# Loads of an attention unit issued one per step of attention

## The chip, the cores and the metric

One core of a Trainium2 chip runs the whole kernel in one launch. The metric is the device time of that launch in microseconds (us); lower is better. The kernel before has a median of 2948.92 us over three runs.

## The reference

One layer of a transformer trunk on 2048 tokens of width 1024, in float32. The changed part belongs to the token mixer:

```python
h = rms_norm(x, g_attn[l]) * (1.0 + scale_a) + shift_a
proj = h @ w_in[l]
q_f, k_f, v_f, q_s, k_s, v_s, f_logit = jnp.split(proj, offsets, axis=-1)
log_f = jax.nn.log_sigmoid((f_logit + b_fgate[l]).astype(jnp.float32))
o_fox = forgetting_attention(...)        # 8 heads of 64: softmax(q.k/8 + F[t] - F[s]), s <= t
o_sb = stick_breaking_attention(...)     # 8 heads of 64: sigmoid(z) * prod of (1 - sigmoid(z)), s < t
mix = jnp.concatenate([head_rms_norm(o_fox, ...), head_rms_norm(o_sb, ...)], axis=-1)
x = x + gate_a * (mix @ w_out[l])
```

Behind it come a gated MLP of inner width 2752 (1024 x 8/3, rounded to 64) with a causal convolution of width 3, and a final RMSNorm. The gates, shifts and scales come from `silu(c) @ w_ada + b_ada`.

## The kernel before

**Precision.** Every operand of a matrix product is split into a high and a low part (fp32r), and a product is three matmuls: high-high, high-low, low-high. A tile therefore has a dimension of two, and most loads carry both parts.

**Units.** Attention is cut into 32 units `(kind, p, tb)`: the kind (`sb`, stick-breaking, then `fox`, forgetting), a pair of heads p from 0 to 3, and a block tb of 512 queries from 0 to 3. A unit needs its own queries Q, and the keys K and values V of its own block and of all earlier blocks of its pair. The units run in that order, one after the other. `attend(...)` is a generator: each of its steps writes one piece of a unit (logits on PE at L596 and L597, the elementwise part on DVE, ACT and POOL, transposes on PE at L606, weighted values on PE at L615). A unit has between 11 and 47 steps.

**Projections.** The projection of a unit (generator `ahead`, function `proj`) reads the eight tiles of normalised input `hs[tb][kt]` from DRAM into tiles named hp (L468, 512 KB each) and multiplies them on PE (L342 for Q and K, L413 for V). In `finish_proj` the results go to DRAM: Q and K into one tensor `qk_...` (L380, L394), V into `vs_...` (L440). Later they are read back by `load_unit` as a unit's tiles: four loads of Q (L362, 256 KB each), four of K (L363, 128 KB each), one of V (L364, 512 KB). The detour through DRAM lays the two parts of both heads out over the partitions as the logits want them. The very first block of the first pair is filled directly.

**Buffers.** Q has 2 buffers, K 5 and V 5. The tiles named hp have 10, shared by the projection's input, by the loads of `w_ada` and by the tiles of its sum.

**Interleaving.** While unit i is attended, `follow(m)` is called at each of its steps m. It advances the projections to a goal that `pace(i)` sets, and once the next unit has been projected it loads that unit. From unit 12 on, `late_mod` is mixed in as well: it loads blocks of `w_ada` (L776), scales them on ACT (L782), sums them on POOL (L783), reduces the sum on PE (L790, L800) and writes one gate to DRAM (`gate_m`, L796).

**What sets the order on each engine.** The kernel is written in the Tile framework, and the context is opened like this:

```python
with _tile.TileContext(nc, schedule_with_timeline_sim=True) as tc:
```

With that option the framework does not issue instructions in program order. A list scheduler with a timeline of its own picks the next instruction of each engine; program order is a priority among those that are ready in that timeline. Only parts that are marked (`fixed()`, `tc.issue_after`) keep a given order. All loads and stores named here are issued by one queue, SP (`nc.sync`), in order: an instruction that waits holds up those behind it. Each DMA on SP also takes one of eight semaphores in turn, so it can be issued only when the DMA eight places ahead of it has landed.

**Names in the profile.** Tiles appear under their names without buffer numbers: `K<-qk_fox` is the load of a K tile, `hp<-hs` a load of the projection's input, `hp<-in_w_ada_dram` a load of w_ada, `os<-oT` the write of a unit's output, `ps_pj`, `ps_qk`, `ps_pt`, `ps_pv` the banks of PSUM for projections, logits, transposes and weighted values.

## Time and profile before

| | us |
|---|---|
| median of three runs | 2948.92 |
| lowest, highest | 2948.36, 2949.31 |
| profiled execution, span from the first to the last instruction | 2941.4 |
| its own total time | not listed |
| PE (matmul) busy | 2867.8 (97%) |
| VectorE (DVE) busy | 2179.5 (74%) |
| ScalarE (ACT) busy | 1686.0 (57%) |
| GpSimd (POOL) busy | 901.1 (31%) |

The span leaves out what lies ahead of the first and behind the last instruction; against the median that is 7.5 us. Rows of the timeline give a start, a duration, the engine (SPq is the SP queue that issues DMAs; its time is the issuing, not the transfer), the line, the operation, the tiles and a count, and in brackets how long the engine had been idle and what ended that. Rows of stretches give for each engine the busy time and the instructions, then the granted clock of PE (1.00 is full), the busy share of the DMA engines and the bytes moved in GB/s.

### The profile page before, as it was taken

Reading aid. Unit: us, or ns where it says so; the run is one execution under the profiler, and the core shown is the slowest. Engines: PE = TensorE matmul, PEld = TensorE weight load, DVE = VectorE, ACT = ScalarE, POOL = GpSimd, SP = SyncE. Lnnn points to the kernel's source line nnn. Section 1 sums busy time; section 2 is a strip of 40 time slices with the busy share of each in tenths; the row PEclk is TensorE's granted clock in tenths of the full one; section 3 lists DMA queues with packets and bytes.
Section 4 is the critical chain, followed back from the end, with each engine's and each line's share of the span. In section 5 each row is a group of like instructions: output and inputs, shape, how many; then the busy total and the mean of one; then the engine's idle time right before and its main releaser. Section 6 shows DMA issues by size and latency. Waiting matters only on the chain.

```text
span 2941.4 us, 45922 instructions
## 1 busy us (share of the span) xinstructions
PE 2867.8 (97%) x15772; PEld 2459.7 (84%) x15772; DVE 2179.5 (74%) x3464; ACT 1686.0 (57%) x3187; POOL 901.1 (31%) x967
## 2 busy tenths in 40 slices
PE   8999999999999999999999999999999999999998
PEld 7888888888988988888888788888788888888887
DVE  5787778877886656658843788888998888575476
ACT  5776767677776656658744554444444445433342
POOL 0431322243032423231213344444254543142200
PEclk8999999999999999999999999999999999999999
DMA  9749756867469794794537775554754444975644
GB/s 293 255 139 321 236 188 207 301 211 229 162 212 356 269 277 139 232 323 140 182 120 233 245 232 128 130 136 129 236 132 125 130 130 132 309 257 185 216 158 151
DMA packets 348346, 601.89 MB, mean 205 GB/s; under 512 B 34672, under 2 KB 178800, under 8 KB 348112
## 3 DMA queue, kind: packets, MB, share of 16 engines
q1 hardware_dynamic: 324208, 558.06, 57.7%
q0 software_dynamic: 10880, 20.97, 4.3%
q10 hardware_dynamic: 13024, 19.93, 1.9%
q8 instruction: 124, 2.03, 0.3%
q14 instruction: 110, 0.90, 0.1%
HBM read 420.77 MB, written 177.02 MB: 203 GB/s over the span
## 4 chain that ended last, share of the span: by engine, by line
PE 46%; DMA 3%; DVE 2%; SPq 1%; ACT 1%; issue 1%; POOL 0%; DVEq 0%; ACTq 0%; POOLq 0%
PE ps_o L1315 19%; PE ps_t L1315 7%; PE ps_o L1614 6%; PE ps_t L1614 3%; PE ps_bc L1614 3%; PE ps_o L912 1%; PE ps_pv L615 1%; DMA r<-rstd 1%; PE ps_bc L912 1%; PE ps_pt L606 1%; PE ps_o L1609 1%; DMA wo<-wos 1%; DMA hm<-hf_m 1%; SPq L895 1%; DVE op L46 1%
## 5 line engine op out<-in xcount | busy, mean ns | idle before, releaser
L1315 PE MATMUL ps_o<-op,wu 128*128 128x512 f32 x2592 | 608.0, 389 | 2.0 <-DVE snap L1366 1.5
L1315 PEld LDWEIGHTS ps_o<-op,wu 128*128 128x128 f32 x2592 | 486.2, 188 | 103.9 <-DVE snap L1366 1.9
L611 DVE TENSOR_TENSOR at<-ps_pt,at 128x512 fp32r<-128x512 f32 (+1 forms) x576 | 366.1, 652 | 100.2 <-ACT at L610 97.3
L636 DVE TENSOR_TENSOR_SCAN a<-r,a 128x512 f32<-128x512 f32 (+2 forms) x320 | 368.3, 1167 | 77.8 <-ACT a L631 39.9
L342 PE MATMUL ps_pj<-hp,w_qk 128*128 128x512 f32 x1512 | 411.2, 403 | 14.5 <-DMA hp<-hs 12.9
L610 ACT ACTIVATE at<-ps_pt 128x512 fp32r<-128x512 f32 (+1 forms) x576 | 318.5, 576 | 139.1 <-PE ps_pt L606 123.1
L615 PE MATMUL ps_pv<-at,V 128*128 128x256 f32 x2216 | 386.8, 292 | 9.3 <-DVE at L611 4.2
L615 PEld LDWEIGHTS ps_pv<-at,V 128*128 128x128 f32 x2216 | 320.9, 190 | 39.8 <-DVE at L611 11.4
L342 PEld LDWEIGHTS ps_pj<-hp,w_qk 128*128 128x128 f32 x1512 | 275.4, 190 | 71.0 <-DMA hp<-hs 16.2
L45 ACT ACTIVATE wu<-wuraw 128x512 fp32r<-128x512 f32 x204 | 128.9, 632 | 248.5 <-PE ps_o L1315 190.1
L596 PE MATMUL ps_qk<-K,Q 128*128 128x512 f32 (+2 forms) x640 | 265.7, 416 | 5.6 <-ACT a L631 3.3
L413 PE MATMUL ps_pj<-w_v,hp 128*128 128x256 f32 (+1 forms) x1536 | 236.6, 288 | 2.1 <-DVE hp L422 1.6
L597 PE MATMUL ps_qk<-K,Q 128*128 128x512 f32 (+2 forms) x640 | 235.7, 369 | 0.0
L1315 PE MATMUL ps_t<-op,wu 128*128 128x512 f32 x888 | 220.8, 390 | 1.0 <-DVE op L46 1.0
L413 PEld LDWEIGHTS ps_pj<-w_v,hp 128*128 128x128 f32 x1536 | 209.0, 189 | 10.9 <-DVE q L373 1.5
L630 ACT ACTIVATE r<-ps_qk 128x512 f32<-128x512 f32 (+2 forms) x320 | 173.1, 541 | 58.2 <-PE ps_qk L597 55.5
L46 DVE TENSOR_TENSOR wu<-wuraw,wu 128x512 fp32r<-128x512 f32 x204 | 189.6, 930 | 18.1 <-ACT wu L45 16.7
L1315 PEld LDWEIGHTS ps_t<-op,wu 128*128 128x128 f32 x888 | 166.4, 188 | 36.5 <-DVE op L46 1.8
L606 PE MATMUL ps_pt<-edge,a 128*128 128x128 f32 x1088 | 185.1, 274 | 8.4 <-DVE a L636 7.8
L1614 PE MATMUL ps_o<-op 128*128 128x512 f32 x840 | 191.5, 389 | 0.0
L1614 PEld LDWEIGHTS ps_o<-op 128*128 128x128 f32 x840 | 157.7, 188 | 32.7
L679 ACT ACTIVATE p<-p,mn 128x128 f32<-128x128 f32 (+15 forms) x128 | 153.9, 1203 | 53.3 <-DVE mn L675 52.2
(342 smaller groups left out, 5237.6 us busy)
## 6 DMA issues: line engine op xcount, KB each, us to landing
hp<-hs SPq DMA_DIRECT2D x224, 512.0 KB
wuraw<-in_w_up_dram SPq DMA_DIRECT2D x80, 512.0 KB
ra<-g SPq DMA_DIRECT2D x136, 256.0 KB
rb<-in_w_down_dram SPq DMA_DIRECT2D x108, 256.0 KB
g<-u SPq DMA_DIRECT2D x80, 256.0 KB
hs<-hp SPq DMA_DIRECT2D x32, 512.0 KB
hp<-in_w_ada_dram SPq DMA_DIRECT2D x32, 512.0 KB
qk_fox<-q SPq DMA_DIRECT2D x32, 512.0 KB
```

Source lines behind the costliest of these rows:

```text
L46: (lo_engine or nc.gpsimd).tensor_sub(lo, src, f(hi))
L342: nc.tensor.matmul(acc, w[kt][:, a, n], h[:, bb], start=kt == 0 and i == 0, stop=kt == KT - 1 and i == 2)
L413: nc.tensor.matmul(av[:, t * width:(t + 1) * width], hts[kt][:, a, tok], w[1][kt][:, bb, 0:width], start=kt == 0 and m == 0, stop=kt == KT ...
L596: nc.tensor.matmul(b[:, :cw], Q[:, hl, 0, qcols], K[:, hl, :cw], start=True, stop=False)
L597: marks.append(nc.tensor.matmul(b[:, :cw], Q[:, hl, 1, qcols], K[:, hl, :cw], start=False, stop=True).ins)
L606: nc.tensor.transpose(b[:, i * P:(i + 1) * P], blk(kts[kk], qi), ident)
L610: copies = [nc.scalar.activation(at[:, 0, lo:], b[:, lo:], AF.Copy).ins, nc.vector.tensor_sub(at[:, 1, lo:], b[:, lo:], f(at[:, 0, lo:])).ins]
L611: nc.vector.tensor_sub(at[:, 1, lo:], b[:, lo:], f(at[:, 0, lo:])).ins]
L615: m = nc.tensor.matmul(o[:, 0:2 * P], V[kt // 4][:, kt % 4, hl, :], rhs, start=first and kk == 0 and w == 0, stop=last and kk == 1 and w == 1)
L636: nc.vector.tensor_tensor_scan(rev, r[:, 0:need][:, ::-1], rev, 0.0 if right[qi] is None else right[qi][:, 0:1], ALU.mult, ALU.add)
L1315: nc.tensor.matmul(b, w[:, p, j], o[:, q], start=first and i == 0, stop=last and i == 2, skip_group_check=True)
L1614: nc.tensor.matmul(b, a[:, p, t * P:(t + 1) * P], w[:, q], start=first and i == 0, stop=last and i == 2, skip_group_check=True)
```

## The change

`load_unit` no longer issues its nine loads. It appends them to a list `arriving`, in the same order as before. A new function `arrive(n)` issues the first n of the list. `follow` calls it at every step: with one load, as long as more than six steps beyond those that the list needs are left in the unit, and with the whole list otherwise.

```diff
@@ load_unit
             for r in range(2):
                 half = slice(r * HD, (r + 1) * HD)
-                nc.sync.dma_start(f(Q[half, h]), src[rows, 0])
-                nc.sync.dma_start(f(K[half, h]), src[rows, 1, r])
-        nc.sync.dma_start(f(V), vs[kind][p][tb])
+                arriving.append((f(Q[half, h]), src[rows, 0]))
+                arriving.append((f(K[half, h]), src[rows, 1, r]))
+        arriving.append((f(V), vs[kind][p][tb]))
         res.append((Q, K, V))
+
+    arriving = []
+
+    def arrive(n):
+        for _ in range(min(n, len(arriving))):
+            nc.sync.dma_start(*arriving.pop(0))
@@ ahead of the loop over the units
     load_unit(*units[0], results["sb", 0])
+    assert not arriving
@@ follow(m), in the loop over the units
             if nxt and projected[1] > i + 1 and loaded_units[0] == i + 1:
                 loaded_units[0] += 1
                 load_unit(*nxt, results[nxt[:2]])
+            arrive(1 if n - m > len(arriving) + 6 else len(arriving))
```

Nothing else is changed. In the kernel after, the three load lines are one, L371, and lines behind it stand 6 to 8 further down (L468 is L474, L596 is L602, L606 is L612, L615 is L621, L740 is L746, L776 is L782, L796 is L802).

**What moves.** Both kernels issue 1775 DMAs on SP. In the schedule, 20 of them stand at another place: five loads of K, five of hp<-hs, three writes at L394, two loads of w_ada, two of the MLP's weights, and one each at L380, L740 and L1443. Of the 252 loads of Q, K and V, the other 247 keep their place. On PE the first 6372 matmuls stand as before, those between 1045.8 and 1332.7 us of the profile before are partly reordered, then again a few between 2104.8 and 2163.9 us.

The first place is SP near 1041 to 1052 us of the profile before, while the first FoX unit is attended. `hs_5`, `hs_6` and `hs_7` are the last three input tiles of a projection that PE is in the middle of; `qk_fox_3_12746` holds the keys of a later unit. Before:

```order
L363 DMA K<-qk_fox_3_12746 64x512 x4
L468 DMA hp<-hs_5_73 128x1024
L468 DMA hp<-hs_6_74 128x1024
L468 DMA hp<-hs_7_75 128x1024
L776 DMA hp<-in_w_ada_dram 128x1024
L363 DMA K<-qk_fox_0_13205 64x512 x4
```

After:

```order
L371 DMA K<-qk_fox_3_12746 64x512 x2
L474 DMA hp<-hs_5_73 128x1024
L371 DMA K<-qk_fox_3_12746 64x512
L474 DMA hp<-hs_6_74 128x1024
L474 DMA hp<-hs_7_75 128x1024
L371 DMA K<-qk_fox_3_12746 64x512
L782 DMA hp<-in_w_ada_dram 128x1024
L371 DMA K<-qk_fox_0_13205 64x512 x4
```

The load of hs_5 has moved ahead of two of the four K loads.

PE at the same place, around the six matmuls that use hs_5 (L342). Before:

```order
L606 MATMUL ps_pt<-edge,p 128x128 x3
L615 MATMUL ps_pv<-at,V 128x256 x5
L596 MATMUL ps_qk<-K,Q 128x384
L597 MATMUL ps_qk<-K,Q 128x384
L596 MATMUL ps_qk<-K,Q 128x512
L597 MATMUL ps_qk<-K,Q 128x512
L342 MATMUL ps_pj<-hp,w_qk 128x512 x6
L606 MATMUL ps_pt<-edge,p 128x128
```

After:

```order
L612 MATMUL ps_pt<-edge,p 128x128 x3
L621 MATMUL ps_pv<-at,V 128x256 x5
L342 MATMUL ps_pj<-hp,w_qk 128x512 x6
L602 MATMUL ps_qk<-K,Q 128x384
L603 MATMUL ps_qk<-K,Q 128x384
L602 MATMUL ps_qk<-K,Q 128x512
L603 MATMUL ps_qk<-K,Q 128x512
L612 MATMUL ps_pt<-edge,p 128x128
```

The six projection matmuls have moved ahead of four logits matmuls.

The second place is SP near 1195 to 1204 us. `hs_7_91` is the last input tile of a projection, `gate_m` is the write of the gate. Before:

```order
L362 DMA Q<-qk_fox_1_14178 64x1024 x3
L363 DMA K<-qk_fox_2_14948 64x512
L796 DMA gate_m<-hp 128x1024
L363 DMA K<-qk_fox_2_14948 64x512
L468 DMA hp<-hs_7_91 128x1024
L364 DMA V<-vs_fox_1_223 128x1024
```

After:

```order
L371 DMA Q<-qk_fox_1_14178 64x1024 x3
L474 DMA hp<-hs_7_91 128x1024
L802 DMA gate_m<-hp 128x1024
L371 DMA K<-qk_fox_2_14948 64x512 x2
L371 DMA V<-vs_fox_1_223 128x1024
```

The load of hs_7 has moved ahead of two K loads and the write of gate_m.

PE at the second place, around the six matmuls that use hs_7. Before:

```order
L606 MATMUL ps_pt<-edge,p 128x128 x4
L615 MATMUL ps_pv<-at,V 128x256 x3
L606 MATMUL ps_pt<-edge,p 128x128 x4
L615 MATMUL ps_pv<-at,V 128x256 x4
L606 MATMUL ps_pt<-edge,p 128x128 x4
L615 MATMUL ps_pv<-at,V 128x256 x5
L606 MATMUL ps_pt<-edge,p 128x128 x3
L342 MATMUL ps_pj<-hp,w_qk 128x512 x6
L615 MATMUL ps_pv<-at,V 128x256 x3
```

After:

```order
L612 MATMUL ps_pt<-edge,p 128x128 x4
L342 MATMUL ps_pj<-hp,w_qk 128x512 x6
L621 MATMUL ps_pv<-at,V 128x256 x3
L612 MATMUL ps_pt<-edge,p 128x128 x4
L621 MATMUL ps_pv<-at,V 128x256 x4
L612 MATMUL ps_pt<-edge,p 128x128 x4
L621 MATMUL ps_pv<-at,V 128x256 x4
L612 MATMUL ps_pt<-edge,p 128x128 x3
```

The six have moved ahead of 23 transposes and value matmuls (11 and 12).

The third place is PE near 1281 to 1288 us, where the projection of a later unit begins; its first four hp loads keep their places on SP. Before:

```order
L615 MATMUL ps_pv<-at,V 128x256 x4
L606 MATMUL ps_pt<-edge,p 128x128 x3
L615 MATMUL ps_pv<-at,V 128x256 x3
L606 MATMUL ps_pt<-edge,p 128x128 x2
L596 MATMUL ps_qk<-K,Q 128x256
L597 MATMUL ps_qk<-K,Q 128x256
L342 MATMUL ps_pj<-hp,w_qk 128x512 x12
L615 MATMUL ps_pv<-at,V 128x256
```

After:

```order
L602 MATMUL ps_qk<-K,Q 128x512
L603 MATMUL ps_qk<-K,Q 128x512
L612 MATMUL ps_pt<-edge,p 128x128 x6
L602 MATMUL ps_qk<-K,Q 128x256
L603 MATMUL ps_qk<-K,Q 128x256
L342 MATMUL ps_pj<-hp,w_qk 128x512 x18
L602 MATMUL ps_qk<-K,Q 128x512
L603 MATMUL ps_qk<-K,Q 128x512
```

The matmuls of the new projection's first three hp tiles, which open the twelve, now stand among the eighteen; 27 matmuls of attention that ran ahead of them (9 transposes, 12 of values, 6 of logits) now run behind them.

Two smaller places have no table here. Near 1062 to 1081 us SP issued a load of w_ada, then the two writes of L380 and L394, another load of w_ada, the write at L740 and eight loads hp<-hs; after, it issues the two writes, the first of those w_ada loads, the write, the other w_ada load and then the hp loads. Near 2105 to 2164 us, at the end of a half of the MLP, DVE and ACT run a few operations in another order.

## The prediction

> **What bounds the kernel now.** The page first: its totals and its chain of waits.

> ```profile
> span 2941.4 us, 45922 instructions
> PE 2867.8 (97%) x15772; PEld 2459.7 (84%) x15772; DVE 2179.5 (74%) x3464; ACT 1686.0 (57%) x3187; POOL 901.1 (31%) x967
> PE 46%; DMA 3%; DVE 2%; SPq 1%; ACT 1%; issue 1%; POOL 0%; DVEq 0%; ACTq 0%; POOLq 0%
> ```

> TensorE works 2867.8 of 2941.4 us; all its idle time is 73.6 us. A changed load order pays or costs only where PE waits for a load. So the second view is what PE waited for (line, wait, us in total, times, longest):

> ```profile
> PE ps_pj L342 <- DMA hp<-hs: 12.9, 8, 6.0
> ...
> PE ps_o L1315 <- DVE snap L1366: 1.5, 1, 1.5
> ...
> PE ps_t L1315 <- DVE op L46: 1.0, 1, 1.0
> ...
> PE ps_qk L596 <- DMA K<-q: 0.7, 1, 0.7
> ...
> PE ps_o L1315 <- DVE op L46: 0.5, 1, 0.5
> ```

> No row has PE waiting for the unit loads of L362 to L364; the one wait for a K is on the first unit, which the projection fills directly. The loads that do make PE wait are hp<-hs, the projection's input, on the same SP queue. The third view, PE in order of time, has two of those waits at 6.01 and 3.40 us, 9.4 of the 12.9:

> ```profile
> 1045.81 0.34 PE L596 MATMUL ps_qk<-K,Q 128*128 128x384 f32 x1
> ...
> 1046.39 0.40 PE L597 MATMUL ps_qk<-K,Q 128*128 128x512 f32 x1
> 1052.80 2.93 PE L342 MATMUL ps_pj<-hp,w_qk 128*128 128x512 f32 x6 [6.01 <-DMA hp<-hs]
> ...
> 1086.71 0.71 PE L342 MATMUL ps_pj<-hp,w_qk 128*128 128x512 f32 x2
> ...
> 1156.69 0.39 PE L596 MATMUL ps_qk<-K,Q 128*128 128x512 f32 x1
> ...
> 1202.54 0.60 PE L615 MATMUL ps_pv<-at,V 128*128 128x256 f32 x3
> ...
> 1208.81 2.93 PE L342 MATMUL ps_pj<-hp,w_qk 128*128 128x512 f32 x6 [3.40 <-DMA hp<-hs]
> ...
> 1280.71 0.39 PE L596 MATMUL ps_qk<-K,Q 128*128 128x512 f32 x1
> ...
> 1284.27 2.91 PE L342 MATMUL ps_pj<-hp,w_qk 128*128 128x512 f32 x12
> ```

> Each wait has a second price, seen in stretches of time (us; busy us of PE, PEld, DVE, ACT, POOL; granted clock; DMA share; GB/s). The first four rows are the waits and what follows them; the others lie on a grid of 3.41 us:

> ```profile
> 1046.79:1052.80 6.01, 0.00 (x1) 0.00 (x0) 0.98 (x5) 1.79 (x5) 1.12 (x2) 0.85 1.04 327
> 1052.80:1057.90 5.10, 5.10 (x16) 4.31 (x17) 0.10 (x1) 0.87 (x2) 0.00 (x0) 0.50 1.05 286
> ...
> 1205.41:1208.81 3.40, 0.00 (x1) 0.00 (x1) 1.46 (x6) 0.51 (x2) 1.07 (x2) 0.89 1.04 340
> 1208.81:1214.89 6.08, 6.08 (x20) 5.46 (x21) 1.57 (x4) 4.40 (x12) 1.88 (x2) 0.50 0.81 310
> ...
> 1047.64:1051.05 3.41, 0.00 (x0) 0.00 (x0) 0.13 (x2) 0.98 (x4) 0.64 (x2) 1.00 1.05 273
> ...
> 1204.65:1208.06 3.41, 0.76 (x7) 0.52 (x5) 2.00 (x7) 1.27 (x3) 1.07 (x2) 1.00 1.03 359
> 1208.06:1211.48 3.42, 2.67 (x6) 2.15 (x7) 0.36 (x1) 0.99 (x4) 0.00 (x0) 0.50 0.97 344
> ...
> 1641.55:1644.96 3.41, 1.82 (x9) 1.16 (x7) 1.52 (x3) 1.86 (x4) 0.40 (x1) 1.00 1.04 384
> 1644.96:1648.37 3.41, 1.79 (x9) 1.45 (x10) 2.29 (x4) 1.18 (x3) 2.03 (x3) 1.00 0.49 156
> ```

> In both waits the DMA engines are full (share 1.04), so bytes set when hp lands. Behind each, PE runs at clock 0.50: 5.10 us of it cost 2.55, 6.08 cost 3.04. A grid window that PE filled 0% or 22% (0.76 of 3.41) is followed by half rate; one filled 53% (1.82) is not; and 78% busy at half rate (2.67 of 3.42) does not yet end it, so it lasts two windows, 6.83 us.

> **The change, part by part.** The same 252 unit loads are issued, of the same size, by the same queue; nothing is added or taken away. What changes is the program order handed to the scheduler. In the schedule that results, 20 of SP's 1775 DMAs stand elsewhere, only five of them unit loads (all K). PE's order is the same for 6372 matmuls, to 1045.7 us, changes until 1332.7, and once more in the MLP at 2104.8 to 2163.9. A lone swap on SP before that (a write and a K load) leaves PE's order as it was, and no row shows PE waiting on a K there: nothing. So the sum has five places. SP around the first two and around 1062 to 1088 (queue row, us on the queue, count):

> ```profile
> 1041.12 4.49 SPq L363 DMA_DIRECT2D K<-qk_fox  x4
> 1045.92 2.54 SPq L468 DMA_DIRECT2D hp<-hs  x3
> ...
> 1050.04 2.38 SPq L363 DMA_DIRECT2D K<-qk_fox  x4
> ...
> 1062.94 0.34 SPq L776 DMA_DIRECT2D hp<-in_w_ada_dram  x1
> ...
> 1067.18 0.32 SPq L394 DMA_DIRECT2D qk_fox<-q  x1
> 1077.19 0.33 SPq L776 DMA_DIRECT2D hp<-in_w_ada_dram  x1
> ...
> 1080.48 7.19 SPq L468 DMA_DIRECT2D hp<-hs  x8
> ...
> 1197.16 0.59 SPq L363 DMA_DIRECT2D K<-qk_fox  x1
> ...
> 1200.74 0.33 SPq L468 DMA_DIRECT2D hp<-hs  x1
> ```

> Place 1 (1046 us). hs_5 passes two of four K loads, 128 KB each. By bytes that is 256 KB at 327 GB/s, 0.8 us; by SP's rows 0.6 per K (2.38 for four), 1.2; with the waits in the first row 1.12 per K, 2.2. I take 1.2, the rows of plain issue. Those K are used at 1156.69 at the earliest, 100 us on, which hides their delay. But PE's order moves too: the four QK matmuls that stood ahead of the projection (1045.81 to 1046.79, 1.0 us) now stand behind it. They covered 1.0 us of the wait, and no longer do. Wait: +1.0 − 1.2 = −0.2 (from +0.2 to −1.2). Half rate: window 1047.64 to 1051.05 stays empty, so it begins at 1051.05 again and ends at 1057.88; hp now lands at 1051.6, so 6.3 us of work run at half rate instead of 5.1, 0.6 more. Should an 84% busy first window end it early, it costs 1.4 instead of 2.55, so −1.1. I take +0.6, because 78% did not end it. Place 1: +0.4 (from −2.3 to +0.8).

> Place 2 (1205 us). hs_7 passes a K, gate_m (512 KB) and a K: 768 KB at 340 GB/s, 2.3 us; by issue times 1200.74 − 1197.16 = 3.6; if gate_m, which waits for other engines, weren't in its way, two K alone, 0.8. I take the bytes, 2.3, as the DMA engines are full. Its six matmuls, however, are moved ahead of 23 others (1202.78 to 1205.41), which covered 2.6 us. Wait: +2.6 − 2.3 = +0.3, 3.7 us in all (−1.0 to +1.8). It now runs from 1202.8 to 1206.5, over two grid windows (edge at 1204.65) that are each idle for 1.85 and busy for 1.55, 45%. That is nearer to the 53% that kept full rate than to the 22% that lost it, so I take the half rate as gone, −3.0, with 0 as the other end. Place 2: −2.7 (from −4.0 to +1.8).

> Place 3 (1284 us), the next projection. The row for SP's waits (queue, releaser, us, times, longest) and the DMA behind it:

> ```profile
> SPq L740 <- DMA hp<-hs: 3.9, 1, 3.9
> ...
> 1283.60 0.32 SPq L740 DMA_DIRECT2D os<-oT  x1
> ```

> The output write at 1283.60 waited for an hp load, so that hp (hs_2) landed then. It feeds the seventh of the twelve matmuls, 1284.27 + 6 x 0.24 = 1285.7, so today it is 2.1 us early. The changed order takes 27 matmuls out from ahead of the twelve; from 1280.71 to 1284.27 those are 3.56 us. The use comes at 1282.15: a new wait of 1.45 us. If the load is issued earlier too, nothing; if all 27 cost somewhat more, 1.8. I take 1.45, the row's own. [...]

> Place 4 (1062 to 1088). Two writes of projected Q and K pass a load of w_ada, which goes 4.5 us later on SP (behind 1067.18 instead of at 1062.94). The next w_ada load waits for POOL to use up the first, and all eight hp loads of the next projection stand behind it. Moved bodily, 1077.19 becomes 1081.7 and hp's first issue 1080.48 becomes about 1082.1. hp is used at 1086.71, which moves to 1085.9. The row of that stretch:

> ```profile
> 1077.00:1082.00 5.00, 5.00 (x40) 4.78 (x40) 3.46 (x10) 3.04 (x7) 2.35 (x5) 1.00 0.56 193
> ```

> DMA is half free (0.56), and 512 KB at 327 GB/s take 1.6 us, so hp lands near 1083.7: hidden, 0. If issue to use must stay the 6.2 us it is today, 2.4 us of wait. It cannot gain: no wait is there.

> Place 5 (2105 to 2164). DVE and ACT work is reordered where a half of the MLP ends; PE's waits there are the three L1315 rows, 1.5 + 1.0 + 0.5 = 3.0. All could go, or as much come; nothing on PE's side tells which. I take 0 (−3.0 to +3.0).

> Sum: +0.4 − 2.7 + 1.45 + 0 + 0 = −0.85 us. It is made against the profiled execution, whose span is 2941.4; its own total isn't listed, and the median of the runs, 2948.92, has 7.5 us around such a span, which the change doesn't touch. Forecast 2948.92 − 0.85 = 2948.1, no change that can be told: 0.2%, 5.9 us, is what a measurement of this kernel can tell.

> **Rivals.** Slower by a fresh wait at place 4. The w_ada load moved 4.5 us back holds up eight hp loads; if hp lands after 1088.4, 2.5 us after its use, a grid window is left only about a quarter busy and half rate follows. Price as at place 1 today, 6.0 + 2.55 = 8.6: 2956.6; at place 2's size, 6.4: 2954.5. For it: one queue, in order, with hp behind a POOL wait. Against: today the stretch is all PE work, no wait, with DMA half free. Chance 0.15.

> Faster: the two hp loads really get ahead, both waits and both half-rate stretches go: −(6.01 + 2.55 + 3.40 + 3.04) = −15.0, 2933.9. If every place came out at its lowest bound, −2.3 − 4.0 − 3.0 = −9.3, 2939.6. For it: hp passes K loads nobody needs for long. Against: PE asks for both hp earlier by nearly what they gain, which forbids the first. Chance 0.12.

> The change does what its words say, loads trickle in and PE waits for Q, K or V: at the 0.7 of the one K wait for each of some 27 units, +19, 2968. Against: only five of 252 loads move, and the K at place 1 has 100 us. Chance 0.02.

> The clock at place 2 stays half: −0.85 + 3.04 = +2.2, 2951.1, by the mechanism that the length of a wait and not its place on the grid decides: 3.40 us cost it today, and 3.7 would again. Chance 0.3, inside "no change". [...]

> **How the numbers follow.** No change holds 0.71 (the sum with either clock, and the places' bounds in part), slower 0.17 (place 4 and late loads), faster 0.12. The range: down to 2942.5, the sum with two thirds of the low bounds; up to 2956.5, place 4's dearer price. Left out are the large gain and the late loads, with what place 5 could add to either.

> **What would show it.** Right: PE still waits for hp<-hs near 1046 (about 5.8) and 1203 (about 3.7); clock 0.50 behind the first alone; a wait of 1 to 2 us near 1282; none at 1086; no row for PE on Q, K or V loads; span 2935 to 2949. Wrong: a wait for hp near 1086 with 0.50 behind it, half rate at 1208 again, no hp wait at 1046, or a difference that comes from outside the changed stretch.

## The result: 0.47% slower, and the profile after

The changed kernel took 2962.15 us (median of five runs) against 2949.31 us for the kernel before on the same chip. The ratio is 1.0047 with a 95% interval of 1.0035 to 1.0059, some 10 to 17 us more. The forecast was 2948.1 with a range to 2956.5. Run again with the experiments the change cost 1.0050 (1.0033 to 1.0068), 14.8 us by the ratio. Four of the executions behind these figures took 20% to 150% longer than the rest and are left out of every figure.

The totals of the page after, and what PE waited for (line, wait, us in total, times, longest). L342, the projection's matmul, keeps its number; the MLP's matmul L1315 is L1323 now.

```profile
span 2964.1 us, 45924 instructions
PE 2874.9 (97%) x15772; PEld 2467.5 (83%) x15772; DVE 2178.4 (73%) x3464; ACT 1686.2 (57%) x3187; POOL 899.9 (30%) x967
```

```profile
PE ps_pj L342 <- DMA hp<-hs: 18.9, 8, 5.2
...
PE ps_o L1323 <- DVE op L46: 4.1, 1, 4.1
```

The wait on hp grew by 6.0 us, from 12.9 to 18.9, and one wait for DVE of 4.1 us is new. There is still no wait for the loads of Q, K and V that the change spreads, so it does not cost by their lateness. PE in order of time shows where the waits are:

```profile
1057.60 2.93 PE L342 MATMUL ps_pj<-hp,w_qk 128*128 128x512 f32 x6 [4.24 <-DMA hp<-hs]
...
1164.89 1.93 PE L342 MATMUL ps_pj<-hp,w_qk 128*128 128x512 f32 x6 [2.83 <-DMA hp<-hs]
...
1217.75 2.93 PE L342 MATMUL ps_pj<-hp,w_qk 128*128 128x512 f32 x6 [5.23 <-DMA hp<-hs]
...
1251.83 1.65 PE L342 MATMUL ps_pj<-hp,w_qk 128*128 128x512 f32 x3 [3.35 <-DMA hp<-hs]
...
2140.03 6.80 PE L1323 MATMUL ps_o<-op,wu 128*128 128x512 f32 x17 [4.11 <-DVE op L46]
```

The first and the third are places 1 and 2 of the prediction. The second, called A from here, and the fourth, called B, are new; in the profile before, PE waited 0.47 us at A and nothing at B. The fifth is place 5, the turn of the MLP. The waits that the prediction set at place 3 (1.45 us near 1282) and rival at place 4 (near 1086) did not come: 0.3 us at place 4, nothing at place 3.

Each of the five is followed by half rate. The same stretches on the 3.41 us grid as in the prediction (us; busy us of PE, PEld, DVE, ACT, POOL; granted clock; DMA share; GB/s), for places 1, A, 2, B and the turn:

```profile
1053.47:1056.88 3.41, 0.00 (x0) 0.00 (x0) 0.69 (x3) 1.00 (x5) 0.39 (x1) 1.00 1.05 269
1056.88:1060.29 3.41, 2.69 (x6) 2.15 (x7) 0.00 (x0) 0.00 (x0) 0.00 (x0) 0.50 1.04 316
...
1162.70:1166.11 3.41, 1.22 (x5) 1.04 (x6) 0.86 (x3) 1.77 (x2) 0.29 (x1) 1.00 0.48 142
1166.11:1169.52 3.41, 3.41 (x15) 3.04 (x14) 0.32 (x1) 1.40 (x3) 0.72 (x1) 0.50 0.00 0
...
1213.89:1217.31 3.42, 0.00 (x0) 0.00 (x0) 0.00 (x0) 0.00 (x0) 0.00 (x0) 1.00 0.99 326
1217.31:1220.72 3.41, 2.97 (x8) 2.39 (x9) 0.66 (x1) 0.60 (x2) 0.00 (x0) 0.50 0.96 255
...
1248.03:1251.44 3.41, 0.45 (x4) 0.21 (x3) 0.98 (x4) 2.28 (x5) 1.50 (x2) 1.00 1.01 393
1251.44:1254.85 3.41, 3.02 (x8) 2.43 (x9) 2.42 (x7) 2.17 (x6) 2.14 (x3) 0.50 1.02 416
...
2135.50:2138.91 3.41, 0.43 (x2) 0.01 (x1) 3.38 (x3) 0.00 (x0) 3.19 (x2) 1.00 0.56 187
2138.91:2142.32 3.41, 2.29 (x5) 1.82 (x6) 3.31 (x6) 1.26 (x2) 0.00 (x0) 0.50 0.98 293
2142.32:2145.73 3.41, 3.41 (x9) 2.64 (x8) 0.25 (x1) 0.00 (x0) 2.68 (x3) 0.50 0.97 372
```

In these rows a window that PE filled for 0.00 to 1.22 us is followed by clock 0.50. As an estimate, half the PE work done at half rate is lost: six matmuls of L342 took 2.93 us at clock 0.50 (1057.60), twelve took 2.91 us at 1.00 (1284.27 in the profile before). Against the profile before, in us:

| place | wait before | wait after | half rate lost before | lost after | difference |
|---|---|---|---|---|---|
| 1 (1057) | 6.01 | 4.24 | 2.55 | 3.05 | -1.3 |
| A (1165) | 0.47 | 2.83 | 0 | 1.7 | +4.1 |
| 2 (1217) | 3.40 | 5.23 | 3.04 | 1.5 | +0.3 |
| B (1251) | 0 | 3.35 | 0 | 1.5 | +4.9 |
| turn (2140) | 1.4 | 4.11 | 0 | 2.85 | +5.6 |

The sum is +13.6, against 12.8 us between the two medians. A second reading needs no estimate: by how much the same matmul of PE's order starts later in the profile after. Over the first reordered stretch (1046 to 1173 us of before, place 1 and A) PE falls behind by 2.4 us, over the second (1202 to 1333, place 2 and B) by 5.6, over the turn by 4.5. That is 12.5 in all, where the table has 2.8, 5.2 and 5.6, so the table's price of the turn is somewhat high. The two profiled spans differ by 22.7 us. Some 6 of that lies ahead of 1004 us, where PE's order is the same in both kernels: the profiled execution of the kernel before was a quick one. Its runs beside the experiments went from 2935 to 2962 us, with a standard deviation of some 4.5 us. A single profile therefore shows a place well and a total badly.

**What stands on the queue at A.** SP's queue (start, us, count), first of the kernel before, then after:

```profile
1151.16 0.34 SPq L468 DMA_DIRECT2D hp<-hs  x1
...
1151.70 2.37 SPq L362 DMA_DIRECT2D Q<-qk_fox  x4
```

```profile
1155.27 2.37 SPq L371 DMA_DIRECT2D Q<-qk_fox  x4
1157.73 0.53 SPq L474 DMA_DIRECT2D hp<-hs  x1
```

The load hs3_6, the projection's seventh input tile for block 3 of FoX pair 2, used to go ahead of the four Q loads of the unit fox 2, block 0 (1 MB); now it goes behind them. The words of the diff do not say so. The swap is there even where the loads of another unit alone are spread (below): the scheduler orders by times that it simulates, and one moved load shifts these for all that follow.

**And at B.** Before, then after:

```profile
1226.92 5.59 SPq L776 DMA_DIRECT2D hp<-in_w_ada_dram  x2
1232.60 5.36 SPq L468 DMA_DIRECT2D hp<-hs  x8
```

```profile
1235.28 9.87 SPq L782 DMA_DIRECT2D hp<-in_w_ada_dram  x2
1245.23 5.23 SPq L474 DMA_DIRECT2D hp<-hs  x8
```

The order of these ten loads is the same, but the two w_ada loads now occupy the queue for 9.87 us, not 5.59. What the second waited for, and for how long (us in total, times, longest), before and then after:

```profile
SPq L776 <- PE ps_pj L413: 5.2, 1, 5.2
```

```profile
SPq L782 <- DMA hp<-in_w_ada_dram: 5.8, 1, 5.8
SPq L782 <- POOL Fd L678: 3.8, 1, 3.8
```

Before, it waited for PE alone. After, it waits for a w_ada load to land (by the times the first of the two, issued at 1235.28 and landed at 1241.4) and then for POOL, which sums until 1244.8. So it seems to get a tile of the sum and no longer one of the projection; which buffer each load takes is not shown. All eight hp loads of the next projection stand behind this load.

**At the turn**, DVE before, then DVE and POOL after:

```profile
2118.89 0.68 DVE L46 TENSOR_TENSOR op<-xh,op 128x512 fp32r<-128x512 f32 x1
2119.60 0.69 DVE L1398 SCALAR_TENSOR_TENSOR u<-u 64x512 f32<-64x512 f32 x1
```

```profile
2133.65 0.69 DVE L46 TENSOR_TENSOR op<-tt,op 128x512 fp32r<-128x512 f32 x1
2134.37 1.67 DVE L1406 SCALAR_TENSOR_TENSOR u<-u 64x512 f32<-64x512 f32 x1
2135.96 1.75 DVE L1407 TENSOR_TENSOR u<-u 64x512 f32<-64x512 f32 x1
2137.74 1.64 DVE L1206 TENSOR_TENSOR tt<-xh 128x512 f32<-128x512 f32 x1
2139.30 0.68 DVE L46 TENSOR_TENSOR op<-xh,op 128x512 fp32r<-128x512 f32 x1
```

```profile
2133.14 2.35 POOL L1245 TENSOR_TENSOR ws<-wuraw 128x512 f32<-128x512 f32 x1 [1.76 <-DMA wuraw<-in_w_up_dram]
2135.57 1.59 POOL L1246 TENSOR_TENSOR wuraw<-wuraw 128x512 f32<-128x512 f32 x1
2137.24 1.59 POOL L1247 TENSOR_TENSOR ws<-wuraw 128x512 f32<-128x512 f32 x1
```

The two operations on the 64-row end piece (L1406, L1407; L1398 and L1399 before) have come ahead of the last split (L46 at 2139.30) for which PE waits. All three between the splits take 1.64 to 1.75 us beside POOL's tensor operations, where the neighbouring splits take 0.68 and 0.69.

### The profile page after: what moved, and what is told of

The parts are those of the page before. It is cut to its first block, busy times and chain, and to the rows that moved or that the text cites. A ratio compares the mean times of both kernels' runs of the same rounds, so it can differ in the third digit from the quotient of the medians.

```text
span 2964.1 us, 45924 instructions
## 1 busy us (share of the span) xinstructions
PE 2874.9 (97%) x15772; PEld 2467.5 (83%) x15772; DVE 2178.4 (73%) x3464; ACT 1686.2 (57%) x3187; POOL 899.9 (30%) x967
## 3 DMA queue, kind: packets, MB, share of 16 engines
q8 instruction: 124, 2.03, 0.3%
## 4 chain that ended last, share of the span: by engine, by line
PE 77%; DMA 11%; DVE 4%; ACT 3%; issue 3%; POOL 2%; SPq 1%; ACTq 0%; DVEq 0%; POOLq 0%
PE ps_o L1323 20%; PE ps_t L1323 8%; PE ps_pj L342 7%; PE ps_o L1622 6%; PE ps_pv L621 6%; PE ps_pt L612 5%; PE ps_pj L419 5%; PE ps_o L918 3%; PE ps_t L1622 3%; PE ps_qk L602 3%; PE ps_bc L1622 3%; PE ps_qk L603 3%; DMA hp<-hs 2%; DMA hp<-in_w_ada_dram 1%; PE ps_bc L918 1%
## 5 line engine op out<-in xcount | busy, mean ns | idle before, releaser
L1323 PE MATMUL ps_o<-op,wu 128*128 128x512 f32 x2592 | 610.9, 390 | 5.6 <-DVE op L46 4.1
L1323 PEld LDWEIGHTS ps_o<-op,wu 128*128 128x128 f32 x2592 | 488.0, 188 | 108.2 <-DVE op L46 4.5
L342 PE MATMUL ps_pj<-hp,w_qk 128*128 128x512 f32 x1512 | 414.9, 405 | 23.1 <-DMA hp<-hs 18.9
L621 PE MATMUL ps_pv<-at,V 128*128 128x256 f32 x2216 | 387.1, 291 | 11.9 <-ACT at L616 5.4
L621 PEld LDWEIGHTS ps_pv<-at,V 128*128 128x128 f32 x2216 | 321.6, 190 | 42.1 <-DVE at L617 10.0
L342 PEld LDWEIGHTS ps_pj<-hp,w_qk 128*128 128x128 f32 x1512 | 276.7, 191 | 78.8 <-DMA hp<-hs 20.7
L602 PE MATMUL ps_qk<-K,Q 128*128 128x512 f32 (+2 forms) x640 | 266.8, 418 | 7.6 <-ACT a L637 3.5
L1323 PE MATMUL ps_t<-op,wu 128*128 128x512 f32 x888 | 220.3, 389 | 0.0
L419 PEld LDWEIGHTS ps_pj<-w_v,hp 128*128 128x128 f32 x1536 | 210.6, 190 | 10.9 <-DVE q L379 1.3
L46 DVE TENSOR_TENSOR wu<-wuraw,wu 128x512 fp32r<-128x512 f32 x204 | 188.6, 925 | 19.1 <-ACT wu L45 17.9
L1323 PEld LDWEIGHTS ps_t<-op,wu 128*128 128x128 f32 x888 | 166.5, 188 | 34.8 <-issue 0.3
L612 PE MATMUL ps_pt<-edge,a 128*128 128x128 f32 x1088 | 185.0, 274 | 7.0 <-DVE a L642 6.5
L685 ACT ACTIVATE p<-p,mn 128x128 f32<-128x128 f32 (+15 forms) x128 | 153.9, 1202 | 64.3 <-DVE mn L681 63.4
```

The source lines that it names most:

```text
L46: (lo_engine or nc.gpsimd).tensor_sub(lo, src, f(hi))
L342: nc.tensor.matmul(acc, w[kt][:, a, n], h[:, bb], start=kt == 0 and i == 0, stop=kt == KT - 1 and i == 2)
L419: nc.tensor.matmul(av[:, t * width:(t + 1) * width], hts[kt][:, a, tok], w[1][kt][:, bb, 0:width], start=kt == 0 and m == 0, stop=kt == KT ...
L602: nc.tensor.matmul(b[:, :cw], Q[:, hl, 0, qcols], K[:, hl, :cw], start=True, stop=False)
L612: nc.tensor.transpose(b[:, i * P:(i + 1) * P], blk(kts[kk], qi), ident)
L621: m = nc.tensor.matmul(o[:, 0:2 * P], V[kt // 4][:, kt % 4, hl, :], rhs, start=first and kk == 0 and w == 0, stop=last and kk == 1 and w == 1)
```

## The experiments

The theory: the time is in a few waits for hp and in the turn, each made by a change of order on SP or DVE, with half rate behind it. The rivals: the spread loads cost by themselves, everywhere; or one place makes it all.

**Which units count.** When the loads are spread in one unit alone, only two units change PE's order: unit 22 (fox 1, block 2, which loads the next unit's tiles) and unit 25 (fox 2, block 1). Each was run alone, and then all the others without these two. The edit of the first; the second has `(25,)`, the third all but 22 and 25:

```diff
     arriving = []
+    SPREAD = (22,)
...
-            arrive(1 if n - m > len(arriving) + 6 else len(arriving))
+            arrive(1 if i in SPREAD and n - m > len(arriving) + 6 else len(arriving))
```

> The loads are spread over the steps in one of the 31 units only, i = 22 (FoX pair 1, block 2; it loads block 3); elsewhere they are issued at once as before. In the built order this gives the changed kernel's order between 1045 and 1173 us and at the MLP turn near 2105 to 2164 us, and the order of before everywhere else. Theory (the time is lost where instructions moved): the two profiles lie 6.1 us apart at 1004 us and 9.7 at 1173, 18.2 ahead of the turn and 22.7 behind it, so this kernel should be slower by 3.6 + 4.5 = 8.1 us, about 2957, with PE waits on hp<-hs near 1046 (4 to 5) and near 1157 to 1165 (2 to 3), and one on a DVE split near 2120 to 2140 (about 4). Rival (half-rate stretches of the clock in the unmoved part, where the profile of the changed kernel is 6 us behind by 1004 us): the time does not follow the moved places, and this kernel is 0 to 3 us slower.

Measured: 2953.1 us, ratio 1.0009 (0.9998 to 1.0020). That is less than the 8.1 us expected, and the times alone do not tell whether this part costs anything.

> The loads are spread only in unit i = 25 (FoX pair 2, block 1; it loads block 2). In the built order this gives the changed kernel's order between 1202 and 1332 us and the order of before elsewhere, the MLP turn included. Theory (the time is lost where instructions moved): the distance of the two profiles grows from 9.7 us at 1173 to 13.6 at 1332, so slower by 3.9 us, about 2953, with PE waits on hp<-hs near 1203 (about 5) and near 1240 (about 3.4, the loads that stand behind two w_ada loads). Rival (clock in the unmoved part): as e1, 0 to 3 us.

Measured: 2954.25, 1.0015 (1.0004 to 1.0027), 4.4 us by the ratio, as expected.

> The loads are spread in all units but i = 22 and i = 25. In the built order one write and one K load near 258 us change places on SP, and nothing else. Theory (the time is lost where instructions moved): no change, within 1 us of before. Rival (the unmoved part is slower in the changed kernel, through the clock or the way it is written): slower by some 5 to 6 us, which the other two then have as well.

Measured: 2947.5, 0.9993 (0.9979 to 1.0007): nothing that can be told. So the loss is that of two units. But the loads of the other units do not really come one per step: in this profile SP's order differs from before by one swap near 258 us, and PE's not at all, since the scheduler's order leaves the loads where they were. What loads that trickle in would cost, no run here shows. Unit 22 brings the waits at A (2.37 us in its profile) and at the turn (4.11); unit 25 brings B (3.08) and lengthens the wait at place 2 (4.15, against 3.40 before).

> The changed kernel itself, timed again beside the next three, to see how large its loss is when more executions are taken (the first comparison had five of each). Theory (time lost at the moved places): the profiles show 3.6 us between 1004 and 1173, 3.9 between 1173 and 1332 and 4.5 at the MLP turn, so 12 us slower, 2960 to 2963. Rival (the two parts alone were 2.7 and 3.8 us slower, and the whole is their sum): 6 to 7 us slower, about 2957.

Measured: 2964.84, 1.0050 (1.0033 to 1.0068), with the same five waits (5.59, 2.40, 3.86, 3.01 and 3.91 us). The rival that expected 6 to 7 us falls. The parts, +2.7 and +4.4 by their ratios, sum to 7; the whole is 14.8. The intervals of the three, taken together, leave about 7 us either way on that difference of 7.7, so it is hardly more than chance. The profiles, one for each kernel, show a reason why the parts could be cheaper. At A unit 22 alone, and the whole change:

```profile
1154.28:1157.70 3.42, 2.57 (x20) 2.12 (x18) 3.42 (x11) 1.19 (x2) 0.00 (x0) 1.00 0.98 201
1157.70:1161.11 3.41, 1.90 (x10) 1.63 (x11) 0.64 (x3) 1.98 (x3) 0.29 (x1) 1.00 0.41 133
```

```profile
1157.19:1160.60 3.41, 1.34 (x6) 1.10 (x7) 1.16 (x4) 1.84 (x3) 0.29 (x1) 1.00 0.51 147
1160.60:1164.01 3.41, 3.41 (x16) 3.12 (x14) 0.51 (x1) 1.39 (x3) 0.72 (x1) 0.50 0.00 0
```

A wait of 2.4 us fell across a grid edge in the first, and PE filled both windows by more than half: no half rate. In the second it fell into one window, 39% busy, and half rate followed. At B it was the same: the wait of 3.08 us in the second part fell across an edge (52% and 58% busy) and cost no clock.

**The turn.** Hold the end piece behind the split for which PE waits:

```diff
-            for fn in held:
-                fn()
+            split_last = nc.cur_bb.bb.instructions[-1]
+            held[0]()
+            with tc.issue_after(split_last):
+                held[1]()
```

> The changed kernel, with one order fixed at the MLP turn: the 64-row end piece (its convolution and its gate on DVE) is queued behind the last operand split of the next half. Theory (at the turn DVE does the end piece first, three of its operations run 2.5 times as long beside POOL, and PE waits 4.1 us for the split behind them, with half rate after it): 4 to 5 us faster than the changed kernel of this job, and no wait of PE on a DVE split over 2 us near 2130. Rival (the turn only moves a wait that comes back later in the half): the same time as the changed kernel.

Measured: 2962.28, 1.0046 (1.0029 to 1.0062). The expected gain did not come, as the rival has it. The wait for DVE is gone and another stands there:

```profile
2139.02 9.20 PE L1323 MATMUL ps_o<-op,wu 128*128 128x512 f32 x32 [5.63 <-DMA wu<-wus]
```

```profile
2121.99 9.05 SPq L1222 DMA_DIRECT2D wuraw<-in_w_up_dram  x6
2131.13 6.30 SPq L1259 DMA_DIRECT2D wu<-wus  x7
```

With the pin the scheduler put all six loads of raw weights ahead of the seven reloads wus, which PE needs first. So the pin was extended to SP:

```diff
+    wus_in = []
...
-            nc.sync.dma_start(f(w).rearrange("p a k n -> p a (k n)"), t)
+            wus_in.append(nc.sync.dma_start(f(w).rearrange("p a k n -> p a (k n)"), t).ins)
...
-                soon.append(load_pair(order[n + 2]))
+                with tc.issue_after(wus_in[-1]) if sblk and n < 2 else nullcontext():
+                    soon.append(load_pair(order[n + 2]))
```

> The changed kernel, with the 64-row end piece at the MLP turn held behind the last operand split on the vector engine, and with the wuraw loads there held on SP's queue behind the seven reloads of wus, which had gone behind six of them when only the first was done. Theory (the turn costs by its longest wait, and the second wait came from SP's order): neither the 4.1 us wait for the vector engine nor the 5.6 us wait for wus is there, and with the half rate behind them 4 to 7 us are won against the whole change: 2956 to 2960. Rival (the turn is held by the bytes themselves or by POOL, whatever their order): a third wait of 3 to 5 us takes the place, 2961 to 2965.

Measured: 2952.42, 1.0016 (1.0003 to 1.0029). PE runs through this part of the turn without a wait; the wait of 1.5 us ahead of it, which the other kernels have too, stays:

```profile
2125.57 8.79 PE L1325 MATMUL ps_o<-op,wu 128*128 128x512 f32 x38
```

By the ratios it is 10 us below the whole change, where 4 to 7 were expected; the two intervals leave some 6 us either way. The wait and its half rate, 4.11 + 2.85 = 7.0, could explain most of it. In this profile the wait at A (2.29 us) also fell across a grid edge, with the two windows filled by 76% and 57%, and cost no clock, which is chance, not the edit.

**A undone.** Hold the four Q loads behind hs3_6 on SP. This gives the turn its old order too. It undoes two things at once, and the turn's new order does not follow from A's swap by itself: with A's swap alone, below, the turn keeps its old order.

```diff
+    def behind_sp(late, early):
+        tc.add_manual_dep(late, early.name, mybir.DependencyInfo(
+            mybir.DependencyClass.NoSync, mybir.DependencyReason.DATA), reason="order on SP")
+    for q in unit_in["fox", 2, 0, "Q"]:
+        behind_sp(q, hp_in["fox", 2, 3, 6])
```

> The changed kernel, with the four Q loads of unit fox2_0 held on SP's queue behind the hp load hs3_6, so that hs3_6 goes ahead of them as in the kernel before. In the program's order this also puts the MLP turn back to what it was before; the eight hp loads at 1240 us stay behind the w_ada load. Theory (the time sits in the few waits on hp and in the turn): the wait at 1155 to 1165 us falls from 2.8 to under 0.5 us, PE's wait for the vector engine at the turn (4.1 us) and the 6.8 us of half rate behind it go, the waits at 1217 and 1251 us stay: 5.1 us of waits gone and up to 4.6 us of half rate, against 15 us for the whole change, so 2953 to 2958. Rival (only the one wait counts, the turn is nothing): 2.3 us less, 2959 to 2963. Rival (the swaps have nothing to do with it, the loads' own lateness costs): 2962 to 2965.

Measured: 2955.34, 1.0019 (1.0004 to 1.0033), 9 us below the whole change. The theory's 2953 to 2958 holds. The rival in which the swaps do not matter falls. The rival of 2959 to 2963, in which the turn is nothing, lies at the end of the interval, which reaches 2960; the run with both pins at the turn speaks against it. A and the turn:

```profile
1158.29 1.65 PE L342 MATMUL ps_pj<-hp,w_qk 128*128 128x512 f32 x6 [0.32 <-DMA hp<-hs]
...
2129.90 0.73 PE L1332 MATMUL ps_t<-op,wu 128*128 128x512 f32 x2 [0.71 <-DVE op L46]
2131.10 6.91 PE L1332 MATMUL ps_o<-op,wu 128*128 128x512 f32 x29 [0.47 <-DVE op L46]
```

By the table above A and the turn are worth 4.1 + 5.6 = 9.7. What remains, 5.6 by the ratio, is put down to B and the rest: B still waits 3.46 us here, with clock 0.50 behind it (1249.28 to 1252.69).

**A alone.** The kernel before, with only this load moved:

```diff
-            nc.sync.dma_start(f(h), hs[tb][kt])
+            with tc.issue_after(q_in["fox", 2, 0]) if (kind, p, tb, kt) == ("fox", 2, 3, 6) else nullcontext():
+                nc.sync.dma_start(f(h), hs[tb][kt])
```

> The kernel before with one load moved: hp hs3_6 goes behind the four Q loads of unit fox2_0 on SP, as the whole change puts it; 27 matmuls around 1155 us shift with it, nothing else. Theory: PE waits 2.4 to 2.8 us there where it waited under 0.5, and half of 3.4 us if the clock falls for one stretch behind it: 2.3 to 4.0 us slower, 2951.5 to 2954. Rival (a wait there is absorbed by the waits at 1205 to 1217 us that follow): within 1 us of before.

Measured: 2953.35, 1.0017 (1.0005 to 1.0030), 1.5 to 9 us slower for one 512 KB load that goes behind 1 MB. The median is 2.7 us above before's. The row:

```profile
1166.95 1.64 PE L342 MATMUL ps_pj<-hp,w_qk 128*128 128x512 f32 x6 [2.21 <-DMA hp<-hs]
```

The wait at place 2 is 3.54 here, as before: A's wait is not absorbed by it. No half rate follows A in this profile: the wait fell across a grid edge, and PE filled the two windows by 82% and 50%. In the six profiles with this swap three lost the clock behind A and three did not, so by the table's method A costs 1.7 to 1.9 us in one execution and 3.6 to 4.1 in another.

**Ways to take hp out from behind the unit loads.** Three were tried. First, each spread load behind the last hp load written so far; second, the same with the loads of a unit together, as in the kernel before; third, all eight hp loads of a projection ahead of its first matmul.

```diff
+            with tc.issue_after(hp_last[-1]) if hp_last else nullcontext():
+                nc.sync.dma_start(*arriving.pop(0))
```

> The changed kernel, and each of the spread loads is queued on SP behind the projection's hp load that the program wrote last before it, in place of the scheduler's choice. Theory (what costs time is hp landing late behind other transfers): the waits of PE on hp<-hs fall below the 18.9 us of the changed kernel and the time comes down to that of before or under it, 2942 to 2952, unless the turn keeps its 4.5 us (then 2947 to 2957). Rival (loads of Q, K and V that come late are what an order on SP must pay for): PE waits for K or Q loads appear, and the time is that of the changed kernel or more.

Measured: 2955.16, 1.0022 (1.0008 to 1.0037), above the theory's 2942 to 2952. The wait for DVE at the turn is gone (1.30 us there for wus, about what stood there before). The waits on hp are 14.6 us: less than the 18.9 of the changed kernel, more than the 12.9 of before. No waits for K or Q of a unit appeared.

```diff
+                with tc.issue_after(hp_last[-1]) if hp_last else nullcontext():
+                    load_unit(*nxt, results[nxt[:2]])
```

> The kernel before (loads of a unit at once), with the nine loads of a unit queued on SP behind the last hp load written before them. Theory (hp landing late is the cost): fewer waits of PE on hp<-hs than the 12.9 us of before, 2 to 8 us faster than before. Rival (hp waits are set by the bytes in flight, not by the place in the queue): 12 to 15 us of hp waits remain, and the time is that of before within 3 us.

Measured: 2948.79, 1.0002 (0.9991 to 1.0013). No gain: the waits on hp are 11.9 us, with 5.28 at place 1 and 3.58 at place 2. That is the rival's forecast: the place in the queue changed, the waits hardly.

```diff
             hts.append(h)
-            accumulate(aq, 0, w[0], h, kt)
+        for kt in range(KT):
+            accumulate(aq, 0, w[0], hts[kt], kt)
             if kt % 2:
```

> The kernel before with all eight hp loads of a projection written ahead of its first matmul, not each ahead of its own; the loads of a unit stay together. It is the other way to take hp loads out from behind K and Q. Theory (the waits on hp come from loads that stand behind other loads of a unit): the waits on hp sum to less than before's, about 12 to 14 us, by 3 to 6 us, and the time falls as much: 2943 to 2947. Rival (ten hp buffers cannot be filled earlier, the loads wait for buffers and then hold SP's queue): waits as before or longer, 2949 to 2955.

Measured: 2963.15, 1.0051 (1.0035 to 1.0066), 15 us slower: a miss. The waits on hp did fall, to 6.2 us, as the theory had it; but the work behind them was ordered anew as well, and PE waits for other engines instead. In this profile PE is idle for 78.6 us, against 73.6 before, and busy for 2880.0 against 2867.8, at a mean granted clock of 0.989 against 0.993.

```profile
PE ps_pv L616 <- ACT at L611: 6.9, 3, 4.6
...
PE ps_pj L342 <- DMA hp<-hs: 6.2, 5, 4.6
PE ps_qk L597 <- DVE mn L676: 5.6, 8, 3.2
```

In every kernel of this study PE stops for 4 to 7 us near place 1 (in this last one the row has ACT as what ended it). The DMA engines are full there in both of these orders (share 1.03); 1040 to 1050 us of the kernel before, and with hp first:

```profile
1040.00:1050.00 10.00, 6.79 (x54) 6.26 (x52) 5.45 (x16) 6.55 (x17) 2.20 (x4) 1.00 1.03 297
```

```profile
1040.00:1050.00 10.00, 6.89 (x54) 6.04 (x52) 5.04 (x14) 4.82 (x15) 0.69 (x2) 1.00 1.03 279
```

**A version that might beat both.** Spread everywhere but in units 22 and 25, with both pins at the turn (the edits above together).

> Two things together, to see whether a version beats both kernels: the loads spread in all units but the two that move the waits (the fox1_3 and fox2_2 loads stay together), and the two pins at the MLP turn (64-row end piece behind the last operand split on the vector engine, wuraw loads behind the reloads of wus on SP). The waits at 1155 and 1245 us should be as in the kernel before (under 0.5 us), the turn should keep its 1.5 us wait and lose the other 1.4, and there should be no half rate behind it. Theory (waits and the half rate behind them make up the time): 1.4 us faster than before by the turn, and up to 2 more if what the spread in the other units alone gave is no chance: 2946 to 2949.5 where before is at 2949 to 2951. Rival (the turn only passes its wait on): a wait of 3 us or more there, or the end later, and 2950 to 2955.

Measured: 2948.6, 0.9996 (0.9977 to 1.0014): no gain that can be told. The 1.4 us at the turn's end are gone, and 1.88 us of wait have come at 2150, where the kernel before had none. No version beat the kernel before.

**Not tried.** B was not undone alone: a w_ada load held behind the eight hp loads would wait for itself, since those loads need buffers that the w_ada work frees. That B's price is its wait and half rate (4.9 us) rests on its rows, on the second part (+1.2 to +8 us with B and place 2 in it) and on what is left when A and the turn are undone.

## Why the prediction was wrong, point by point

**"PE waits for no unit load; so only hp matters": right.** After the change, too, no row has PE wait for a Q, K or V of a spread unit. The rival of loads that come late, 2968, is 5.9 us from the measured time, about as near as the rival of place 4, 2956.6; its mechanism did not occur, since nearly all unit loads keep their place.

**"So the sum has five places": the step that failed.** Twenty DMAs move on SP, and the prediction priced the hp loads that got ahead of others, but not the one that fell behind. That hs3_6 goes behind four Q loads could be read from the order. By the prediction's own method, 1 MB at 327 to 340 GB/s is 3.1 to 3.2 us, and by SP's rows four Q issues are 2.4 us; the wait measured 2.2 to 2.8 in the six profiles with the swap. A was worth +4.1 in the profile after; alone it cost 5.0 by the ratio, 2.7 by the medians. B, whose mechanism the prediction had for another place, is the other term that the sum lacks: +4.9 by the rows.

**Place 5: 0 taken, +5.6 by the rows, +4.5 by the matmuls' starts.** The prediction saw that DVE work was reordered at the turn and gave up on it: "nothing on PE's side tells which". The order on DVE's side did tell: two operations had come ahead of the split for which PE waits. The bounds of 3.0 us either way were also too narrow. They priced PE's present waits and not the moved operations at their longer duration, 1.67 and 1.75 us (the profile before has 2.32, 1.78 and 1.76 us for DVE operations at this turn), nor the half rate behind.

**Place 4's rival: right mechanism, wrong place.** A projection's hp loads stood behind a w_ada load that waited for another to land and for POOL to use it up, as the rival has it, but at 1245 us and not at 1086. The 0.15 given to it was for one spot. A w_ada load is followed by eight hp loads at more than one projection, and the changed order altered what the load at B waits for (PE for 5.2 us before; a load for 5.8 and POOL for 3.8 us after). The price put on the mechanism, 6.4 to 8.6 us, was somewhat high: 4.9.

**Place 2: the wait forecast +0.3, measured +1.8 in that profile (+0.4 to +1.8 over the kernels with this order); half rate forecast gone, found.** The hp load did leave earlier against its use: issued at 1206.88 with PE stopping at 1212.52. But it took 10.9 us to land, 8.1 before. The DMA engines were full: the windows 1210.48 to 1213.89 and 1213.89 to 1217.31 have shares of 1.05 and 0.99, the second with PE wholly idle. The prediction took 2.3 us off the landing for the bytes passed on the queue; measured against PE's work the load landed only 0.8 us earlier. That bytes already under way still set it would fit, but no run shows it apart. On the clock the input was wrong: the longer wait left a whole window empty, so half rate came. Even with its own input, two windows filled by 45%, half rate was the likelier outcome, by the counts below. It ended after one window, not two, because PE filled that window for 2.97 of 3.41 us, against 2.67 before.

**Place 1: +0.4 forecast, -1.3 by the table.** The wait lost 1.8 us in the profile after (0.4 to 2.0 over the kernels that have this order), and half rate stayed. Small either way.

**Place 3: +1.45 forecast, nothing found.** By what SP waited for next, the third hp load took 8.5 us to land, not the 12.7 of before, and was there 3.7 us ahead of its use. The sum had kept its landing where it was. It also counted no half rate for a wait of 1.45 us; the one nearest to it in the profile before, 1.52 us ahead of 2083.60, left PE busy for 1.90 of 3.42 us in its window (2081.87 to 2085.29), and the clock stayed at 1.00 in the next.

**Around the span.** The prediction held 7.5 us to lie between the profiled span and the run's time. The profile after has 2964.1 us of span in a run of 2965.82: 1.7. The rest was that the profiled run of before was quick. It did not move the forecast, which used the difference alone.

**The chances.** Slower had 0.17, all of it on place 4 and on late loads. With one missed swap, one reordered engine taken at zero and a mechanism counted at one spot of several, that was too little. (Two thirds of the low bounds give a lower end of 2942.7, not 2942.5.)

## What to carry to other kernels

When a change reorders a shared queue, list both directions, what gets ahead and what falls behind, for every load that PE waits for soon. Price the second as fully as the first: bytes ahead, the wait, and the half rate that follows a window left mostly empty (here, every one filled by 43% or less). Where work is reordered on another engine ahead of something that PE needs, read that engine's order to the operation PE waits for, rather than put zero on it. Pin only with the next reader in view: two of the pins at the turn freed one wait and let the scheduler make another, 5.6 and 1.9 us long.

## What the hardware showed that was not expected

- A stall of 2.4 us, shorter than a window, cost half rate or not by where it fell on the 3.41 us grid: 2.40 us did with a window filled by 39% (the whole change run again), 2.37 us did not with windows filled by 75% and 56% (unit 22 alone). By the counts above the line is at a window about half filled by PE. Half rate ended after every window filled by 86% or more and went on after every one filled by 79% or less. It comes in ordinary stretches too: the window at 313.77 us of the profile before is 66% filled and keeps the clock, the one at 312.77 of the profile after is 37% filled and loses it; at 1641.55 before it is 53%, kept, at 1661.04 after 28%, lost. The two profiles of the changed kernel have 13 and 10 windows at half rate, so this may be a part of the scatter of 4.5 us between runs of one kernel.
- Three DVE tensor operations at the turn of the profile after, each with two inputs in SBUF (L1406, L1407 and L1206), took 1.67, 1.75 and 1.64 us while POOL's L1245 to L1247 ran. In the profile before the same three (L1398, L1399 and L1198) took 0.68 to 0.69 us, with POOL idle from 2117.82 to 2123.68. In another row POOL's time was the longer one: the split at 2133.65 kept its 0.69 us inside POOL's L1245, which took 2.35 us where the two behind it took 1.59. One operation with an input in PSUM kept its 0.68 us while POOL's ran (the row below, from the kernel with both pins at the turn, where POOL's L1247 runs from 2124.87 to 2127.02).

```profile
2124.87 2.15 POOL L1247 TENSOR_TENSOR ws<-wuraw 128x512 f32<-128x512 f32 x1
```

```profile
2125.80 0.68 DVE L1349 TENSOR_TENSOR y<-ps_o,snap 128x512 f32<-128x512 f32 x1
```

- With the DMA engines full (shares 0.99 to 1.05), an earlier place on the queue bought little in the one case here: the load at place 2 was issued 3.6 us earlier against PE's work and took 2.8 us longer to land.
